# Wide high-part products in runs of eight, and activation slots 32 bytes longer, in a split-fp32 decoder trunk

## The chip, the cores and the metric

The kernel runs on one core of a Trainium2 chip. The metric is the time of one execution on the device in microseconds, as the median of several runs. The kernel before the change was run three times: 1990.41, 1990.26 and 1989.77 us, median 1990.26.

## What is computed

One recurrent layer (RG-LRU) and one sliding-window attention layer with sinks, each followed by a SwiGLU feed-forward block, over a residual stream of 256 tokens by 2048 features in float32. Nearly all the arithmetic is in matrix products of the activations (256 tokens) with weights:

```
h = rms_norm(x, g1);  y, xb = split(h @ lru_w_in)           # 2048 x 4096
xb = conv4(xb);  r, i = sigmoid(blockdiag(xb))               # 8 blocks of 256 x 256, twice
x = x + (lru_scan(r, i, xb) * gelu(y)) @ lru_w_out           # 2048 x 2048
x = x + (silu(gate) * up) @ ffn_w_out                        # 2048 x 11264, 5632 x 2048
k, v = split(rms_norm(x) @ w_kv)                             # 2048 x 512
x = x + attention(rms_norm(x) @ w_q, k, v, sinks) @ w_o      # 2048 x 2048, twice
x = x + (silu(gate) * up) @ ffn_w_out                        # second feed-forward block
```

## The kernel before, in words

**Layout.** Activations are kept transposed: features on the 128 partitions, the 256 tokens along the free axis, so a feature tile is 128 x 256. Weights are the stationary operand, 128 x 128 at a time, and activations stream past them as the moving operand.

**Split products.** To come near float32 with the one-pass type float32r, every operand is split in a high part, rounded to float32r, and a low part, the rest. A product is then three: weight high by activation high, weight high by activation low, weight low by activation high. A split activation lies in a *slot* of 512 columns: the high part in columns 0 to 255, the low part in 256 to 511. There are 58 slots, allocated one after the other in the same pool (`slot`, L138), and handed out and taken back in a queue. Other 256-wide temporaries use slots too.

**Jobs.** Weights come in blocks of 128 x 1024 float32 (512 KB): two feature tiles (k = 0, 1) by four output tiles (f = 0 to 3). One block is one job. `stream` (L271) walks the list of all jobs: it loads a block four jobs ahead on SyncE's queue into one of four `raw` buffers (L241), splits it three jobs ahead into `hi` on ScalarE (L259) and `lo` on VectorE (L260), again with four buffers each, and issues the job's products on TensorE. 688 of the jobs are jobs of `group` (L340); 8 are gate jobs with their own loop (L641) and 8 are K/V jobs (L832 to L843).

**Products of a job.** `group` makes a list of (k, f, part), and `products` (L289) issues it at L323, or at L321 where the product is to be held behind other matmuls. Parts are named in `PARTS` (L287):

```
PARTS = {"h": (1, 0, 2 * T), "a": (1, 0, T), "b": (1, T, 2 * T), "l": (0, 0, T)}
```

Part a is weight high by the slot's high half and b by its low half, both 256 wide and summed into the same 256 columns of a PSUM bank. Part h is both at once, 512 wide: it needs the whole bank, the two halves of which are added when the bank is evicted. Part l is weight low by the high half. So a job has 24 narrow products, or 16 if all a and b are taken as h. A bank that takes an h part is called *two* here. In each group two of the four banks are two (three in the query projection, `wide=3`; none where `sync` is empty or the group is *paired*, which is so for 16 jobs of the attention's output projection, where two output tiles share a bank).

**Order.** In before, most products are a, b and l. `products` takes three h parts in a row at certain jobs of a group (`SYNC`, L63), at its start, and after matmuls of other kinds (`pe_other`, L327, which norms, scores and transposes go through; `RUNS`, `since` and `due`, L301 to L314). The last job of a group goes output tile by output tile, so that banks finish one after the other. In the middle of a job, and at its end, `half_tick` and `run_bg` issue steps of the background work (evictions' further steps, norms, gates, softmax), as far as a running estimate of the time of VectorE and ScalarE allows.

**Evictions.** `pull` (L387) and `residual` (L469) take a bank. If it is two, ScalarE copies the second half to a temporary (L113, `t<-b`) and VectorE adds it to the first (L122); otherwise one operation of VectorE or ScalarE does. At the end of the kernel the residual tiles are stored as they are finished (L481).

Of the kernel before, what the change touches and what calls it, by code (L numbers as in the profile page):

```python
# [17 lines left out]
P = 128  # L18
D = 2048
T = 256  # L20
# [20 lines left out]
class Val:  # L41


    def __init__(self, ap=None):
        self.ap = ap
        self.ready = False


class Trunk:
# [11 lines left out]
    DEBT = 2500.0  # L61
    WARM = 15
    SYNC = (0, 2, 5)  # L63
    RUNS = 3
    DVE_TICK = 640.0
    ACT_TICK = 800.0

    def __init__(self, ctx, tc, dram):
        self.tc, self.nc, self.d = tc, tc.nc, dram
        nc = self.nc  # L70
        const = ctx.enter_context(tc.tile_pool(name="const", bufs=1))
        psum = ctx.enter_context(tc.tile_pool(name="psum", bufs=1, space=bass.MemoryType.PSUM))
        tmp = ctx.enter_context(tc.tile_pool(name="tmp", bufs=1))
        self.tmp = tmp
        self.par = const.tile([P, NPAR], F32, name="par")
        self.con = const.tile([P, NCON], F32, name="con")
        self.cc = const.tile([P, 32], F32, name="cc")
        self.x = [const.tile([P, 4, T], F32, name=f"x{i}") for i in range(4)]
        self.slots = deque(range(58))
        self.spool = const  # L80
        self.held = {}
        self.raw = [const.tile([P, 1024], F32, name=f"raw{i}") for i in range(4)]
        self.hi = [const.tile([P, 1024], F32R, name=f"hi{i}") for i in range(4)]
        self.lo = [const.tile([P, 1024], F32R, name=f"lo{i}") for i in range(4)]
        self.banks = deque(psum.tile([P, 512], F32, name=f"b{i}") for i in range(8))
        self.misc = 0
        self.started = False
        self.xin = 0
        self.other = None
        self.runs = 0  # L90
        self.since = 0
        self.hold = False
        self.tmps = deque(const.tile([P, T], F32, name=f"t{i}") for i in range(4))
        self.halves = deque(const.tile([P, T], F32, name=f"h{i}") for i in range(8))
        self.rstd = [const.tile([P, T + 2], F32, name=f"rstd{i}") for i in range(2)]
        self.acc = const.tile([P, T], F32, name="acc")
        self.sq = deque(const.tile([P, T], F32, name=f"sq{i}") for i in range(2))
        self.jobs = []
        self.bg = deque()
        self.tick = -2 * self.LD  # L100
        self.dve = 0.0
        self.act = 0.0
# [36 lines left out]

    def slot(self, dt=F32R):  # L140
        i = self.slots.popleft()
        s = self.spool.tile([P, 2 * T], dt, tag=f"s{i}", name=f"s{i}")
        self.held[id(s)] = (i, s)
        return s

# [143 lines left out]
    def products(self, todo, st, hi, lo, x2, last, keep=False, paired=False):  # L289

        ps, begun = st["ps"], st["begun"]
        rest, half, n = list(todo), len(todo) // 2, 0
        ticked = False
        while rest:
            if not ticked and n >= half and not (self.since == 0 and rest[0][2] == "h"):
                self.half_tick()
                ticked = True  # L300
            if self.other is not None:  # L301
                self.runs = self.RUNS
            if not keep and self.runs and rest[0][2] != "h":
                left = set(rest)
                run = [(k, f) for k in range(2) for f in range(4) if ps[f][1] and (k, f, "a") in left
                       and (k, f, "b") in left][:3]
                new = ps[rest[0][1]][1] and ps[rest[0][1]][2] not in begun
                due = self.other is not None or self.since % 3 == 1 and self.since > 3
                if len(run) == 3 and (new or due and ps[run[0][1]][2] in begun):
                    self.runs -= 1  # L310
                    rest = [(k, f, "h") for k, f in run] + [q for q in rest if q[:2] not in run or q[2] == "l"]
            k, f, p = rest.pop(0)
            n += 1 + (p == "h")
            self.since = 0 if p == "h" else self.since + 1  # L314
            high, c0, c1 = self.PARTS[p]
            w = (hi if high else lo)[:, k * 512 + f * P:k * 512 + f * P + P]
            args = (ps[f][0][:, 0:c1 - c0], w, x2[k][:, c0:c1])
            kw = dict(start=ps[f][2] not in begun, stop=last and all(q[1] != f for q in rest), skip_group_check=paired)
            if self.other is not None and p == "h":
                with self.tc.issue_after(self.other):  # L320
                    self.nc.tensor.matmul(*args, **kw)  # L321
            else:
                self.nc.tensor.matmul(*args, **kw)  # L323
            self.other = None
            begun.add(ps[f][2])
# [14 lines left out]
    def group(self, src, nk, xs, done, last=False, sync=(), paired=False, jobs=None, wide=2):  # L340

        st = {}
        jobs = self.jobs if jobs is None else jobs
        both = [(k, f) for k in range(2) for f in range(4)]
        for c in range(nk // 2):
            def mm(hi, lo, c=c):
                if c == 0:
                    if paired:  # L350
                        ps = [self.bank() for _ in range(2)]
                        st["ps"] = [(ps[f // 2][:, f % 2 * T:f % 2 * T + T], False, f // 2, f % 2) for f in range(4)]
                        st["bank"] = ps
                    else:
                        ps = [self.bank() for _ in range(4)]
                        st["ps"] = [(p, bool(sync) and f < wide, f, 1) for f, p in enumerate(ps)]
                        st["bank"] = ps
                    st["begun"] = set()
                    self.hold = False
                elif c >= nk // 2 - 2:  # L360
                    self.hold = True
                x2 = [self.need(xs[2 * c + kt]) for kt in range(2)]
                keep = not self.started
                if keep:
                    self.started = True
                    todo = [(k, f, p) for k in range(2) for q in ("ab", "l") for f in range(4)
                            for p in ("h" if q == "ab" and k == 0 and f < 2 else q)]
                elif c == nk // 2 - 1:

                    todo = [(k, f, p) for f in range(4) for k in range(2) for p in "abl"]  # L370
                else:
                    if c in sync:
                        self.runs = max(self.runs, 1)

                    two = [f for f in range(4) if st["ps"][f][1]]
                    one = [f for f in range(4) if f not in two]
                    order = [(one, "ab"), (one, "l")] + [(two, q) for q in (("ab", "l") if c == 0 else ("l", "ab"))]
                    todo = [(k, f, p) for g, q in order for k in range(2) for f in g for p in q]
                self.products(todo, st, hi, lo, x2, c == nk // 2 - 1, keep, paired)
                if last:  # L380
                    for q in x2:
                        self.free(q)
                if c == nk // 2 - 1:
                    done([(p, two, st["bank"][b] if last_of else None) for p, two, b, last_of in st["ps"]])
            jobs.append((src(c), mm))

    def pull(self, bank, o=None, r=None):  # L387
# [743 lines left out]
```

## Time and profile before

| | |
|---|---|
| median of the three runs | 1990.26 us |
| span of the profiled execution, first to last instruction | 1988.6 us |
| TensorE busy | 1982.0 us, 16684 matmuls |
| VectorE busy | 1271.2 us |
| ScalarE busy | 1067.9 us |
| weights and inputs read | 371.88 MB, 188 GB/s over the span |

The profile is of one execution. PE stands for TensorE's matmuls, PEld for its weight loads, DVE for VectorE, ACT for ScalarE and SP for SyncE; L323 is line 323 of the kernel. A row of a group names line, engine and operation, the output and inputs by the program's names (numbers left out), the shape and the count; behind the bar stand its busy time in us, the mean ns of one, and the idle time of the engine just before. In a row of a stretch (two times from the span's start, with a colon) stand its length, then for each engine the busy time and the number of instructions, and the granted clock (1.00 is full). In a row of the timeline stand the start in us, the time from the first start to the last end, and the count of like instructions in a row. Matmuls are pipelined: the duration of one is its latency, and the next starts long before it ends.

### The profile page before, as it was taken

To read this page: it belongs to the slowest core of one execution; us is meant where nothing else is said; L and a number is where in the kernel's file an instruction comes from. 1 tells how busy PE (TensorE), PEld (TensorE's weight loads), DVE (VectorE), ACT (ScalarE), POOL (GpSimd) and SP (SyncE) were. 2 spreads that over 40 slices of the span, in tenths; PEclk is the share of its full clock that TensorE was granted. 3 is DMA by queue.
4 is the path that set the end of the run, shared out by engine and by line. 5 is a ranking of instruction groups with operands and counts; after the bars stand their busy time and mean duration, and the time that the engine had idled before them with its cause. 6 is when DMAs were issued, how large, how long until landed. Compare 5 with 4: busy or idle time off the path is not lost.

```text
span 1988.6 us, 40066 instructions
## 1 busy us (share of the span) xinstructions
PE 1982.0 (100%) x16684; PEld 1935.5 (97%) x16684; DVE 1271.2 (64%) x2049; ACT 1067.9 (54%) x1624; POOL 0.2 (0%) x4
## 2 busy tenths in 40 slices
PE   9999999999999999999999999999999999999999
PEld 9999999999999999999999889999999999999999
DVE  8988876556556655545668786755565565554453
ACT  7798655444444444444556775544454454444442
POOL 0000000000000000000000000000000000000000
PEclk9999999999999999999999999999999999999999
DMA  8555655565556555556555435565566656656663
GB/s 279 185 187 182 211 191 192 196 196 191 192 195 196 191 192 196 195 191 194 197 186 167 134 101 163 188 197 195 191 193 196 195 191 194 197 193 203 204 208 128
DMA packets 105302, 376.58 MB, mean 189 GB/s; under 512 B 11808, under 2 KB 14240, under 8 KB 105120
## 3 DMA queue, kind: packets, MB, share of 16 engines
q1 hardware_dynamic: 104832, 373.88, 57.8%
q8 instruction: 130, 2.13, 0.4%
q14 instruction: 52, 0.43, 0.1%
q10 hardware_dynamic: 288, 0.14, 0.0%
HBM read 371.88 MB, written 2.10 MB: 188 GB/s over the span
## 4 chain that ended last, share of the span: by engine, by line
PE 99%; ACT 0%; DVE 0%; DMA 0%; issue 0%; ACTq 0%
PE b L323 94%; PE b L334 2%; PE b L641 1%; PE b L331 1%; PE b L832 1%; ACT s L113 0%; PE b L321 0%; PE b L841 0%; PE b L842 0%; PE b L843 0%; DMA x<-in_x 0%; DVE s L131 0%; DVE lo L260 0%; ACT L113 0%; DVE s L122 0%
## 5 line engine op out<-in xcount | busy, mean ns | idle before, releaser
L323 PE MATMUL b<-s,hi 128*128 128x256 f32 (+1 forms) x10276 | 1431.9, 285 | 0.4 <-ACT s L113 0.4
L323 PEld LDWEIGHTS b<-s,hi 128*128 128x128 f32 x10276 | 1313.4, 188 | 30.4 <-ACT s L113 0.7
L260 DVE TENSOR_TENSOR lo<-raw,hi 128x1024 fp32r<-128x1024 f32 (+1 forms) x705 | 861.4, 1223 | 651.2 <-ACT hi L259 648.1
L259 ACT ACTIVATE hi<-raw 128x1024 fp32r<-128x1024 f32 (+1 forms) x705 | 745.7, 1059 | 817.7 <-PE b L323 756.7
L323 PE MATMUL b<-s,lo 128*128 128x256 f32 x5504 | 831.8, 277 | 0.0
L323 PEld LDWEIGHTS b<-s,lo 128*128 128x128 f32 x5504 | 720.4, 188 | 2.4 <-issue 0.8
L113 ACT ACTIVATE s<-h 128x256 fp32r<-128x256 f32 (+1 forms) x106 | 40.8, 411 | 23.8 <-DVE h L122 23.8
L113 ACT ACTIVATE t<-b 128x256 f32<-128x256 f32 x136 | 49.8, 374 | 2.5 <-PE b L323 0.3
L113 ACT ACTIVATE s<-x,par 128x256 fp32r<-128x256 f32 x80 | 38.6, 499 | 19.3 <-DVE x L122 13.6
L113 ACT ACTIVATE s<-s 128x256 f32<-128x256 f32 (+1 forms) x112 | 39.6, 409 | 5.7 <-DVE s L126 5.5
L113 ACT ACTIVATE h<-h 128x256 f32<-128x256 f32 (+1 forms) x104 | 38.8, 375 | 2.1
L113 ACT ACT_TABLE_LOAD x30 | 38.5, 1283 | 0.5
L126 DVE SCALAR_TENSOR_TENSOR s<-x,par,s 128x256 fp32r<-128x256 f32 x80 | 37.5, 482 | 1.4 <-ACT s L113 0.8
L122 DVE TENSOR_TENSOR h<-b,rstd 128x256 f32<-128x256 f32 x100 | 37.6, 417 | 0.0
L122 DVE TENSOR_TENSOR x<-x,b 128x256 f32<-128x256 f32 x64 | 24.1, 418 | 21.0 <-PE b L323 21.0
L113 ACT ACTIVATE s<-s,h 128x128 f32<-128x128 f32 x64 | 28.3, 443 | 13.3 <-DVE h L131 13.2
L122 DVE TENSOR_TENSOR h<-h,rstd 128x256 f32<-128x256 f32 x94 | 35.4, 419 | 0.0
L122 DVE TENSOR_TENSOR h<-h,h 128x256 f32<-128x256 f32 x88 | 35.0, 420 | 0.4 <-ACT h L113 0.4
L122 DVE TENSOR_TENSOR s<-h,s 128x256 fp32r<-128x256 f32 x88 | 35.2, 420 | 0.1
L122 DVE TENSOR_TENSOR h<-b,t 128x256 f32<-128x256 f32 x92 | 34.6, 417 | 0.0
L122 DVE TENSOR_TENSOR s<-s,s 128x256 fp32r<-128x256 f32 (+1 forms) x80 | 30.9, 422 | 3.5 <-ACT s L113 3.5
L334 PE MATMUL b<-s,s 64*128 64x256 f32 (+3 forms) x292 | 29.0, 302 | 0.1
(99 smaller groups left out, 566.4 us busy)
## 6 DMA issues: line engine op xcount, KB each, us to landing
raw<-in_ffn_in SPq DMA_DIRECT2D x352, 512.0 KB, 3.5
raw<-in_ffn_out SPq DMA_DIRECT2D x176, 512.0 KB, 4.3
raw<-in_lru_in SPq DMA_DIRECT2D x63, 512.0 KB, 3.6
raw<-in_lru_out SPq DMA_DIRECT2D x32, 512.0 KB, 3.7
raw<-in_w_q SPq DMA_DIRECT2D x32, 512.0 KB, 3.3
raw<-in_w_o SPq DMA_DIRECT2D x32, 512.0 KB, 3.3
raw<-in_gate SPq DMA_DIRECT2D x8, 512.0 KB, 3.9
raw<-in_kv SPq DMA_DIRECT2D x8, 512.0 KB, 4.3
```

The lines of the kernel that those rows point to most:

```text
L113: self.nc.scalar.activation(out, in_, func, **kw)
L122: self.nc.vector.tensor_tensor(out, a, b, op)
L126: self.nc.vector.scalar_tensor_tensor(out, a, s, b, op0, op1)
L259: self.nc.scalar.activation(hi[:, q], raw[:, q], AF.Copy)
L260: self.nc.vector.tensor_tensor(lo[:, q], raw[:, q], hi[:, q].bitcast(F32), ALU.subtract)
L323: self.nc.tensor.matmul(*args, **kw)
L331: self.other = self.ins(f(*args, **kw))
L334: self.other = self.ins(f(*args, **kw))
L641: nc.tensor.matmul(out[j], (hi if high else lo)[:, c:c + P], x2[kt][:, q:q + T], start=kt == 0 and high > q, stop=kt == 1 and not high)
L832: nc.tensor.matmul(ps[f][:, 0:T], w0, x2[kt][:, q:q + T], start=k0 + kt == 0 and high > q, stop=k0 + kt == ND - 1 and not high)
```

## The change

All banks of groups that aren't paired become two, all their a and b parts become h parts, and a job issues its eight h parts first (k = 0 for the four output tiles, then k = 1) and then its eight l parts in the same order. The last job of a group goes output tile by output tile, two h and two l each. The runs of three and what decided on them are gone. A slot is allocated 520 columns long, of which 512 are used, so that slots lie 2080 bytes apart instead of 2048. The half-tick comes after half of the list, now eight h parts.

```diff
@@ class Trunk
-    RUNS = 3
+    STEP = 8
@@ slot
-        s = self.spool.tile([P, 2 * T], dt, tag=f"s{i}", name=f"s{i}")
+        w = self.spool.tile([P, 2 * T + self.STEP], dt, tag=f"s{i}", name=f"s{i}")
+        s = w[:, 0:2 * T]
@@ products
-            if not ticked and n >= half and not (self.since == 0 and rest[0][2] == "h"):
+            if not ticked and n >= half:
                 self.half_tick()
                 ticked = True
-            if self.other is not None:
-                self.runs = self.RUNS
-            if not keep and self.runs and rest[0][2] != "h":
-                left = set(rest)
-                run = [(k, f) for k in range(2) for f in range(4) if ps[f][1] and (k, f, "a") in left
-                       and (k, f, "b") in left][:3]
-                new = ps[rest[0][1]][1] and ps[rest[0][1]][2] not in begun
-                due = self.other is not None or self.since % 3 == 1 and self.since > 3
-                if len(run) == 3 and (new or due and ps[run[0][1]][2] in begun):
-                    self.runs -= 1
-                    rest = [(k, f, "h") for k, f in run] + [q for q in rest if q[:2] not in run or q[2] == "l"]
             k, f, p = rest.pop(0)
-            n += 1 + (p == "h")
-            self.since = 0 if p == "h" else self.since + 1
+            n += 1
@@ group
-                        st["ps"] = [(p, bool(sync) and f < wide, f, 1) for f, p in enumerate(ps)]
+                        st["ps"] = [(p, True, f, 1) for f, p in enumerate(ps)]
...
-                    todo = [(k, f, p) for k in range(2) for q in ("ab", "l") for f in range(4)
-                            for p in ("h" if q == "ab" and k == 0 and f < 2 else q)]
+                    todo = [(k, f, p) for k in range(2) for p in "hl" for f in range(4)]
+                elif paired:
+                    todo = [(k, f, p) for q in ("ab", "l") for k in range(2) for f in range(4) for p in q]
                 elif c == nk // 2 - 1:
-                    todo = [(k, f, p) for f in range(4) for k in range(2) for p in "abl"]
+                    todo = [(k, f, p) for f in range(4) for p in "hl" for k in range(2)]
                 else:
-                    if c in sync:
-                        self.runs = max(self.runs, 1)
-                    two = [f for f in range(4) if st["ps"][f][1]]
-                    one = [f for f in range(4) if f not in two]
-                    order = [(one, "ab"), (one, "l")] + [(two, q) for q in (("ab", "l") if c == 0 else ("l", "ab"))]
-                    todo = [(k, f, p) for g, q in order for k in range(2) for f in g for p in q]
+                    todo = [(k, f, p) for p in "hl" for k in range(2) for f in range(4)]
```

More of the change, by code (lines that the diff above doesn't have):

```diff
@@ L89, in __init__ @@
         self.other = None
-        self.runs = 0
-        self.since = 0
         self.hold = False
```

## The prediction

> **What bounds the kernel now.** I read the page first (busy shares, granted clock, chain), then TensorE's waits, then the matmul groups with their shapes kept apart, and then single stretches. The forecast hangs on the pitch, the time from one product's start to the next, and no group states it.
>
> ```profile
> span 1988.6 us, 40066 instructions
> PE 1982.0 (100%) x16684; PEld 1935.5 (97%) x16684; DVE 1271.2 (64%) x2049; ACT 1067.9 (54%) x1624; POOL 0.2 (0%) x4
> PEclk9999999999999999999999999999999999999999
> PE 99%; ACT 0%; DVE 0%; DMA 0%; issue 0%; ACTq 0%
> ```
>
> TensorE is busy for the whole span at full clock, and 99% of the chain that ended last is TensorE. This is what it waited for, in total:
>
> ```profile
> PE b L334 <- DVE s L131: 1.7, 3, 1.0
> PE b L268 <- DVE lo L265: 1.2, 1, 1.2
> PE b L323 <- ACT s L113: 0.4, 1, 0.4
> ```
>
> It waited 3.3 us in 1988.6, so no wait is there to be removed: the time can change only if the matmuls take more or less time, or if the change makes new waits. The matmuls by shape:
>
> ```profile
> L323 PE MATMUL b<-s,hi 128*128 128x256 f32 x9570 | 1291.3, 277 | 0.4 <-ACT s L113 0.4
> L323 PE MATMUL b<-s,lo 128*128 128x256 f32 x5504 | 831.8, 277 | 0.0
> L323 PE MATMUL b<-s,hi 128*128 128x512 f32 x706 | 201.6, 393 | 0.0
> ```
>
> The 277 ns of a narrow product is its latency, not its pitch: they overlap. For the pitch I take stretches that hold nothing but narrow products:
>
> ```profile
> 157.00:183.00 26.00, 26.00 (x223) 26.00 (x222) 22.49 (x43) 24.13 (x48) 0.00 (x0) 1.00 0.57 185
> 1890.00:1980.00 90.00, 90.00 (x797) 90.00 (x796) 41.29 (x38) 34.63 (x34) 0.00 (x0) 1.00 0.55 177
> ```
>
> A product is counted if any of its 277 ns falls into the stretch, which is 277/113, some 2.4 products too many. So 90.00/794.6 = 113.3 ns, and 26.00/220.6 = 117.9 ns. Clock and shape are the same in both: there is a **short rhythm** of 113.3 and a **long rhythm** of 117.9, 4.6 ns apart, and each holds for many products in a row. Which one holds can be seen to depend on where the operands start. In the shared K/V projection, L832 streams an activation slot past weights 12 times, and then L841 to L843 stream weights past an activation slot 12 times:
>
> ```profile
> 1013.80 0.39 PE L832 MATMUL b<-s,hi 128*128 128x256 f32 x2
> ...
> 1015.16 0.28 PE L841 MATMUL b<-hi,s 128*128 128x256 f32 x1
> ...
> 1016.58 0.40 PE L832 MATMUL b<-s,hi 128*128 128x256 f32 x2
> ...
> 1018.00 0.28 PE L841 MATMUL b<-hi,s 128*128 128x256 f32 x1
> ...
> 1019.37 0.39 PE L832 MATMUL b<-s,hi 128*128 128x256 f32 x2
> ...
> 1020.73 0.28 PE L841 MATMUL b<-hi,s 128*128 128x256 f32 x1
> ...
> 1022.14 0.40 PE L832 MATMUL b<-s,hi 128*128 128x256 f32 x2
> ```
>
> The first column is the start in us. Twelve products take 1.36, 1.42, 1.42, 1.37, 1.36, 1.41 us, that is 113, 118, 118, 114, 113, 118 ns each. Each time the moving operand goes from slot to weight tile the rhythm flips, and going back it stays: half of this stretch is in the long rhythm. As allocated, every slot starts 32 bytes past a multiple of 512 and every weight tile 480 past one. In the L323 products all moving operands lie at one offset, and there the rhythm holds.
>
> **The change part by part.** *Wide instead of two narrow.* Of the 688 jobs of L323, the 672 that aren't paired now issue 8 wide and 8 narrow low products: 5376 wide ones in place of 10752 narrow or fewer (719 are wide already: 706 above and, by the built program, 13 at L321). A pair costs 2 x 113.3 = 226.6. The latency of a wide product is 393 - 277 = 116 ns more than that of a narrow one; if the added columns cost as much in the pitch, a wide one takes 113.3 + 116 = 229.3 ns. Two places check this, three wide and two narrow products up to the start of the next piece, in the short and in the long rhythm:
>
> ```profile
> 361.90 1.07 PE L323 MATMUL b<-s,hi 128*128 128x512 f32 x5
> 362.81 0.39 PE L323 MATMUL b<-s,lo 128*128 128x256 f32 x2
> ...
> 185.76 1.10 PE L323 MATMUL b<-s,hi 128*128 128x512 f32 x5
> 186.69 0.52 PE L323 MATMUL b<-s,lo 128*128 128x256 f32 x3
> ```
>
> (0.91 - 2 x 0.1133)/3 = 228 ns, and (0.93 - 2 x 0.1179)/3 = 231 ns. I take 229.3, which lies between: +2.7 each, 5376 x 2.7 = 14.5 us, less 719 x 2.7 = 1.9 paid already: **+12.6 us**. The bounds: above, a wide product as slow as two in the long rhythm, 235.8; below, no row shows columns streamed faster than in the short rhythm, so I mirror the one difference that the trace shows and let a wide product save 4.6 on its pair, 222.0, or, further out, 4.6 on each of its halves, 217.4.
>
> Runs of three is all that the trace has. What the fourth to eighth do, it doesn't show; the bounds hold that too.
>
> *Slots 2080 bytes apart instead of 2048.* The moving operand's offset now takes 16 values in 512 bytes, and it changes four times in a job, between the two feature tiles of the high and of the low products and to the next job. No row shows an offset of 32 bytes to another slot; the nearest are the K/V rows, where a change of offset left half the products in the long rhythm. I take that half for all narrow products that remain with a slot as an operand: 5504 low ones, 256 of the paired jobs, 192 at L641, 192 of K/V, together 6144. 6144 x 0.5 x 4.6 = **+14.1 us**; ends: none in the long rhythm (0) and all (28.3). What is in it now has to come off. Most of it lies early:
>
> ```profile
> 20.00:320.00 300.00, 300.00 (x2519) 295.20 (x2518) 257.96 (x471) 223.17 (x377) 0.00 (x0) 1.00 0.61 197
> L323 PE MATMUL b<-s,hi 128*128 128x512 f32 x101 | 28.7, 392 | 0.0
> ```
>
> (The second row is of the same stretch.) 300.00 - 2519 x 0.1133 - 101 x 0.116 = 2.9 us: **-3 us**.
>
> *Evictions.* All four banks of a group now carry two halves, where it was two or three of four: about 137 more copies on ScalarE and as many adds on VectorE.
>
> ```profile
> L113 ACT ACTIVATE t<-b 128x256 f32<-128x256 f32 x136 | 49.8, 374 | 2.5 <-PE b L323 0.3
> L122 DVE TENSOR_TENSOR x<-x,b 128x256 f32<-128x256 f32 x64 | 24.1, 418 | 21.0 <-PE b L323 21.0
> ```
>
> That is 137 x 0.374 = 51 us on ScalarE (54% busy) and 137 x 0.42 = 58 us on VectorE (64%), spread over the span beside matmuls. The tightest place is the stretch 20 to 320 above: VectorE is busy 258 of 300 us, and eight groups with two more adds each bring 16 x 0.42 = 6.7 us against 42 us of idle time. I cost it at nothing; with that cover gone it would be those 7 us. Only the end has nothing beside it. The last group had single halves, and its last product was followed by one add:
>
> ```profile
> 1985.18 0.28 PE L323 MATMUL b<-s,lo 128*128 128x256 f32 x1
> 1985.49 0.42 DVE L122 TENSOR_TENSOR x<-x,b 128x256 f32<-128x256 f32 x1 [0.26 <-PE b L323]
> ```
>
> Now ScalarE copies the second half during that add (374 under 418 ns), and a second add follows: **+0.4 us** before the last store. Removed runs of three, the later half-tick (after 8 of 16 products, two thirds of a job) and the dropped order after other matmuls move background work by less than a job; weights, loads and queues stay as they are, and nothing waits for them now: 0.
>
> *Sum:* 12.6 + 14.1 - 3 + 0.4 = +24.1. The span was 1988.6, and the median of the runs, 1990.26, lies 1.7 above it: 1988.6 + 24.1 + 1.7 = **2014 us**. Own range: 228 and none in the long rhythm give 5376 x 1.4 - 1.9 - 3 + 0.4 = +3, 1993; 235.8 and all in it give 5376 x 9.2 - 1.9 + 28.3 - 3 + 0.4 = +73, 2063. Since neither end goes with the other term's middle, I cut it to 2003 to 2042.
>
> **The rivals.** *A: a toll per product, which the padding and the width take away.* If the 113.3 holds a fixed cost for each start, a wide product pays it once; and if the equal offsets are what keeps narrow products at 113.3 or 117.9, spreading them may help. With a toll of 4.6, wide 222.0, narrow all at 113.3: -5376 x 4.6 = -24.7, -1.9 (the 719 of now), -3, +0.4 = -29, **1961 us**; with the toll gone from narrow ones too it is lower, by up to 28 us. With the other terms as forecast (14.1 - 1.9 - 3 + 0.4 = 9.6 us) it decides once a wide product comes below 226.6 - 1.8 = 224.8 ns. For it speaks that offsets matter at all; against it 393 - 277 = 116, more than a narrow pitch, and the rows of three wide ones. The Trainium skill, TensorE: Matmul & The Clock Gate, section Back-to-back issue gap, speaks for it: an isolated warm product takes its columns at 2.4 GHz and 2.5 ns on top, so 215.8 ns wide and 109.2 narrow. By the difference alone, 2.5 ns a pair, the estimate would be -13.4 us, 1977; this trace's narrow pitch of 113.3 doesn't agree with that page's figure.
>
> *B: the padding does nothing.* Wide at 229.3, narrow all at 113.3: 12.6 - 3 + 0.4 = +10, **2000 us**. Against it, the K/V rows; for it, that a step of 32 bytes isn't the step seen there. The Trainium skill, SBUF — State Buffer, section Who interferes with whom, says that TensorE never waits for anyone there, by which offsets would be free: B again, and the K/V rows disagree with it.
>
> *C: a long rhythm throughout.* Every change of offset breaks the short rhythm and eight narrow products are too few to find it: wide 235.8, narrow 117.9, **2063 us**. For it: the long rhythm held for 220 products once it was there.
>
> That the edit doesn't do what it says can be left out: the built program has the 5376 wide products and the 2080-byte step.
>
> **How the numbers follow.** Forecast 0.38, A 0.33, B 0.17, C 0.06, and 0.06 that the terms cancel, within 0.2% (about what a measurement of this kernel can tell from no change, here 4 us). So slower 0.38 + 0.17 + 0.06 = 0.61, same 0.06, faster 0.33. The range leaves out most of C and the deeper part of A, where narrow products gain too, some 0.06 and 0.13: 1948 to 2042.
>
> **What would show it.** In the profile after, TensorE stays at 100% with waits of a few us. The wide group has about 5367 rows at L310 and some at L308. A stretch inside an FFN gives the job's pitch: now 24 x 113.3 = 2.72 us; by the forecast 8 x 229.3 + 8 x 115.6 = 2.76; by A 2.68; by B 2.74; by C 2.83. The low products of one job alone tell the rhythm: 0.91 us for eight at the short pitch, 0.94 at the long one. ScalarE's t<-b group grows from 136 to about 270. The forecast is wrong if the job is below 2.72, or if the added time lies in TensorE's waits instead of its pitch.

## The result and the profile after

The changed kernel takes 2042.64 us (median of 4 runs, 2042.49 to 2042.81) against 1990.3 us before: 1.0262 times the time, 95% interval 1.0248 to 1.0277. The forecast was 2014 us in a range of 1948 to 2042, so the sign was right and the added time, 52 us instead of 24, twice what was forecast and just outside the range. The page of the changed kernel, answering to the first lines of before:

```profile
span 2041.0 us, 31024 instructions
PE 2032.5 (100%) x12027; PEld 1776.5 (87%) x12027; DVE 1324.0 (65%) x2193; ACT 1104.7 (54%) x1761; POOL 0.2 (0%) x4
PEclk9999999999999999999999999999999999999999
```

TensorE is busy throughout at full clock as before. Its waits, in total:

```profile
PE b L321 <- DVE s L129: 1.7, 3, 1.0
PE b L267 <- DVE lo L264: 1.2, 1, 1.2
PE b L310 <- DVE s L124: 1.1, 1, 1.1
PE b L318 <- ACT h L111: 0.3, 1, 0.3
PE b L318 <- DVE s L120: 0.2, 1, 0.2
```

That is 4.5 us where it was 3.3: no engine became a new bound, and the time went into the products themselves. The groups by shape (L310 is now the products' line) show the 5367 wide and 5504 narrow low products, each some ns longer than in before (395 and 281 ns, where it was 393 and 277):

```profile
L310 PE MATMUL b<-s,hi 128*128 128x512 f32 x5367 | 1392.0, 395 | 1.1 <-DVE s L124 1.1
L310 PE MATMUL b<-s,lo 128*128 128x256 f32 x5504 | 796.4, 281 | 0.0
```

As before, the pitch says more than the duration. In the timeline of TensorE inside a feed-forward block each job is two pieces:

```profile
601.84 2.02 PE L310 MATMUL b<-s,hi 128*128 128x512 f32 x8
603.70 1.13 PE L310 MATMUL b<-s,lo 128*128 128x256 f32 x8
604.66 2.03 PE L310 MATMUL b<-s,hi 128*128 128x512 f32 x8
606.53 1.10 PE L310 MATMUL b<-s,lo 128*128 128x256 f32 x8
607.47 2.03 PE L310 MATMUL b<-s,hi 128*128 128x512 f32 x8
```

From start to start: 1.86 and 1.87 us for eight wide products, 233 ns each, and 0.96 and 0.94 us for eight narrow ones, 119 ns each. A job is 2.81 us, where 24 products of 113.3 took 2.72.

Taken from start to start over the whole trace, without the steps that hold a wait or a matmul of another kind, the mean pitch is:

| | narrow, ns | wide, ns | above 113.3 and 226.7, us in all |
|---|---|---|---|
| before | 113.7 | 229.5 | 5.0 + 2.0 = 7.0 |
| after | 117.9 | 232.4 | 27.6 + 30.5 = 58.1 |

The last column is what all products together take beyond the short rhythm, narrow ones first. It grew by 51.1 us, 22.6 on the narrow and 28.5 on the wide products. With 0.9 us at the end (below) that is 52.0 of the 52.4 us between the two spans, 1988.6 and 2041.0. So nearly the whole loss is pitch.

### The profile page after: what moved, and what is told of

Its sections match the earlier page's. It is cut to its first block, busy times and chain, and to the rows that moved or that the text cites. A ratio compares the mean times of both kernels' runs of the same rounds, so it can differ in the third digit from the quotient of the medians.

```text
span 2041.0 us, 31024 instructions
## 1 busy us (share of the span) xinstructions
PE 2032.5 (100%) x12027; PEld 1776.5 (87%) x12027; DVE 1324.0 (65%) x2193; ACT 1104.7 (54%) x1761; POOL 0.2 (0%) x4
## 5 line engine op out<-in xcount | busy, mean ns | idle before, releaser
L310 PE MATMUL b<-s,hi 128*128 128x512 f32 (+1 forms) x5623 | 1426.7, 390 | 1.1 <-DVE s L124 1.1
L310 PEld LDWEIGHTS b<-s,hi 128*128 128x128 f32 x5623 | 979.6, 188 | 163.2 <-DVE s L124 1.4
L310 PEld LDWEIGHTS b<-s,lo 128*128 128x128 f32 x5504 | 774.4, 188 | 79.6 <-issue 0.8
L310 PE MATMUL b<-s,lo 128*128 128x256 f32 x5504 | 796.4, 281 | 0.0
L111 ACT ACTIVATE t<-b 128x256 f32<-128x256 f32 x280 | 103.4, 380 | 89.4 <-PE b L310 57.9
L120 DVE TENSOR_TENSOR h<-b,t 128x256 f32<-128x256 f32 x192 | 80.1, 419 | 0.9 <-ACT t L111 0.3
L120 DVE TENSOR_TENSOR h<-h,rstd 128x256 f32<-128x256 f32 x194 | 77.0, 420 | 1.5
L881 DVE CUSTOM_DVE_ANT_0 s<-b,con,par 128x128 f32<-128x128 f32 x64 | 27.1, 473 | 0.0
```

The lines of the kernel that those rows point to most:

```text
L111: self.nc.scalar.activation(out, in_, func, **kw)
L120: self.nc.vector.tensor_tensor(out, a, b, op)
L881: nc.vector.tensor_tensor_reduce(sc[hh][:, c0:c1], ps[hh][:, c0:c1], con[:, K_MASK + c0:K_MASK + c1], rr[:, b * 8 + f * 2 + hh:b * 8 + f * ...
```

## The experiments

Four theories were tested. Runs are called by the first part of their label, e1 to e16. **P**: changes of the operand's offset between products, which the padding brings, throw the products out of the short rhythm. **W**: a run of eight wide products costs by itself. **D**, formed after the first runs: the pitch hangs on the distance between the start of the moving operand and that of the weights, modulo 256 bytes. **M**, at first and then as M2: wide products go round a cycle of three pitches, and what rhythm follows depends on the count modulo three. Each run stands beside runs of the kernel before on the same chip.

**Width alone.**

```diff
-    STEP = 8          # of the changed kernel
+    STEP = 0
```

> The change without its padding: slots 2048 bytes apart again, all high-part products wide, eight and eight. Theory P (the offsets that vary from slot to slot throw the products out of the short rhythm): narrow pitch back to 113.3 ns, wide near 229, time about 2000 us. Theory W (a run of eight wide products costs by itself and leaves the narrow ones behind it in the long rhythm, whatever the offsets): wide 231 to 233 ns, narrow 117 to 118, time 2030 to 2045 us.

Measured: 2012.8 us, 1.0113 (1.0098 to 1.0128). The two theories each missed: the time lies between them. Its timeline shows why:

```profile
605.02 2.00 PE L310 MATMUL b<-s,hi 128*128 128x512 f32 x8
606.86 1.07 PE L310 MATMUL b<-s,lo 128*128 128x256 f32 x8
607.76 1.99 PE L310 MATMUL b<-s,hi 128*128 128x512 f32 x8
609.59 1.11 PE L310 MATMUL b<-s,lo 128*128 128x256 f32 x8
610.53 1.31 PE L310 MATMUL b<-s,hi 128*128 128x512 f32 x5
```

Eight narrow products take 0.90 us in one job (113 ns) and 0.94 in the next (118 ns), by turns. Of some 580 whole jobs half have a narrow mean of 113 to 114 ns and half one of 117 to 119, and the wide ones go 226, 229, 232 ns, over and over, 229.0 in the mean. Products beyond the short rhythm: 27.7 us, so +20.7 against before; the spans differ by 2010.6 - 1988.6 = 22.0.

**Padding alone.**

```diff
-        s = self.spool.tile([P, 2 * T], dt, tag=f"s{i}", name=f"s{i}")
+        w = self.spool.tile([P, 2 * T + 8], dt, tag=f"s{i}", name=f"s{i}")
+        s = w[:, 0:2 * T]
```

> The kernel before with nothing but the padding: slots 2080 bytes apart, products in the old order. P: narrow pitch about 118 ns in all L323 products, 15,000 x 4.6 ns = 69 us more, about 2055 us. W: the old time within 5 us, 1990 us.

Measured: 2060.43 us, 1.0353 (1.0337 to 1.0368): P's number, and W as the only cause is out. Narrow products have 118.1 ns in the mean. In the order of before, the padding costs 70 us.

**One common offset, another one.**

```diff
+        self.gap = const.tile([P, 8], F32, name="gap")   # 32 bytes ahead of the slots
```

> The kernel before with 32 unused bytes ahead of the slots: all slots still 2048 bytes apart and at one common offset, but 64 instead of 32 bytes past a multiple of 512, while the weight tiles stay at 480. If only a change of offset between products costs (P in its plain form): short rhythm as before, 113.3 ns, 1990 us. If the common offset itself sets the pitch: the narrow pitch moves as a whole, to anything between 108 and 118 ns, 1910 to 2055 us.

Measured: 2088.91 us, 1.0495 (1.048 to 1.0511). All slots still lie at one common offset here, and it is the slowest run of all, so P in its plain form falls: the offset itself matters. A stretch of 55 us near the end that holds only narrow products, in before and in this run:

```profile
1925.00:1980.00 55.00, 55.00 (x488) 55.00 (x487) 25.20 (x25) 20.44 (x20) 0.00 (x0) 1.00 0.51 166
```

```profile
2025.00:2080.00 55.00, 55.00 (x461) 55.00 (x460) 20.83 (x17) 18.05 (x17) 0.00 (x0) 1.00 0.44 144
```

These are 488 products against 461; less the 2.4 that reach in from before, 113.3 and 119.9 ns.

Traffic of the other engines isn't the reason. In the whole trace of this run a narrow product takes 119.8 ns in the mean where neither VectorE nor ScalarE runs beside it (2340 of them) and 120.0 where both do (3551); it takes 119.9 where no DMA packet is under way (3044) and 119.9 where more than twelve are (7232).

**Steps of 64 bytes.** `STEP = 16` in the changed kernel, with one temporary less of two kinds to make room.

> The change with slots 2112 bytes apart, a step of 64 bytes instead of 32 (one temporary fewer of two kinds to make room). P with any change of offset harmful: as the changed kernel, 2035 to 2050 us. P with only odd multiples of 32 bytes harmful: narrow near 113.3, wide near 229, about 2000 us. W: 2030 to 2045 us.

Measured: 2039.24 us, 1.0246 (1.0229 to 1.0263), as with 32 bytes. Odd multiples of 32 bytes aren't what is wrong.

**Weights and slots moved together**, the 32 bytes of e3 ahead of both (before `raw` in the list of tiles):

> The kernel before with 32 unused bytes ahead of weights and slots alike: slots 64 and weight tiles 0 past a multiple of 512, so that their distance stays what it was. If the distance between the moving operand's offset and the weights' sets the pitch: 113.3 ns and 1990 us as before. If the slots' own offset does (64 past, as in the run before in which they alone were moved and the narrow pitch was 120.4 ns): 120 ns and 2085 to 2090 us.

Measured: 1990.49 us, 1.0001 (0.999 to 1.0011). Moved by the same 32 bytes together with the weights, the slots cost nothing: the absolute offset doesn't matter, the distance between the two operands does. **Other distances**, the gap of e3 with other lengths:

> The kernel before with all slots moved by 256 bytes, to 288 past a multiple of 512; weights at 480. In the run with nothing but the padding, the products with a slot at 288 were the shortest (116.6 ns mean, 113 at the shortest quarter). If the pattern repeats every 256 bytes and only changes between products kept them from the short rhythm: 113.3 ns, 1990 us. If the distance to the weights matters in the whole 512 bytes: another pitch, 116 to 121 ns, 2030 to 2090 us.

> The kernel before with all slots moved by 448 bytes, to 480 past a multiple of 512, the same offset as the weights. By the runs so far no theory names a number; if every distance but the old one costs, 117 to 121 ns and 2040 to 2090 us. A pitch under 113 ns would show that the old distance is not the best one and give a version that beats both.

> The kernel before with all slots moved by 128 bytes: 160 past a multiple of 512, weights at 480, so 192 bytes behind the weights' offset modulo 256 where it was 64. So far a distance of 64 gave 113.3 ns, 0 gave 119.9 and 96 gave 120.4. Theory D (the pitch hangs on this distance modulo 256): any one pitch for the whole run; in the shared K/V projection, where the operands change roles and the distance is 192 too, both 113 and 118 ns were seen, so 113.3 and 1990 us is the likeliest, 118 and 2060 us the other end.

> The kernel before with all slots moved by 64 bytes, distance 128 modulo 256. Distances of 0, 96 and 192 gave 119.9, 120.4 and 117.8 ns, 64 gave 113.3. Theory D says one pitch for the run without naming it; 117 to 121 ns, 2050 to 2090 us, if 64 is the only good distance. If the padding's 70 us are the mean over the eight distances, the eight base runs must average near 2060 us; a mean well below it would leave a price for the changes themselves.

> The kernel before with all slots moved by 96 bytes, distance 160 modulo 256. As in the run with distance 128: 117 to 121 ns, 2050 to 2090 us, if 64 is the only good distance; below 113 ns if there is a better one.

> The kernel before with all slots moved by 160 bytes, distance 224 modulo 256. As in the run with distance 128: 117 to 121 ns, 2050 to 2090 us, if 64 is the only good distance; below 113 ns if there is a better one.

> The kernel before with all slots moved by 224 bytes, distance 32 modulo 256. As in the run with distance 128: 117 to 121 ns, 2050 to 2090 us, if 64 is the only good distance; below 113 ns if there is a better one.

In before, slots start at 32 and weights at 480 past a multiple of 512, a distance of 64 modulo 256. With the mean pitch of a stretch of 55 us of narrow products near the end, counted as above:

| distance mod 256, bytes | run | median, us | pitch, ns |
|---|---|---|---|
| 0 | e7 | 2087.25 | 119.9 |
| 32 | e16 | 2045.22 | 116.6 |
| 64 | before, e5, e6 | 1990.3 to 1990.5 | 113.3 |
| 96 | e3 | 2088.91 | 119.9 |
| 128 | e13 | 2070.49 | 118.6 |
| 160 | e14 | 2051.59 | 117.4 |
| 192 | e9 | 2054.09 | 117.9 |
| 224 | e15 | 2064.78 | 118.4 |

Two of the expectations are missed: for a distance of 192 the likeliest was said to be 1990 us, and e16 lies below its 2050. The pitch is a mean: at 64 every step of the stretch takes 112 to 114 ns, at 96 they vary from 116 to 125.

The row of e6, 256 bytes on, is that of before again, and that of e16 is the nearest of the others:

```profile
1925.00:1980.00 55.00, 55.00 (x488) 55.00 (x487) 25.27 (x25) 20.44 (x20) 0.00 (x0) 1.00 0.54 166
```

```profile
1980.00:2035.00 55.00, 55.00 (x474) 55.00 (x473) 23.18 (x20) 19.11 (x18) 0.00 (x0) 1.00 0.49 161
```

D holds: moved by 256 bytes, 0.9999 (0.9989 to 1.001); moved by anything else that was tried, 1.0275 or more. Of the eight distances that the padding's steps of 32 bytes produce, the kernel before sits on the only one at 113.3. None lies below it, so no layout among these gives a version that beats before. The mean of the eight medians (with 1990.3 for 64) is 2056.6 us; padding alone measured 2060.4. So the sum agrees with the mean of the distances to about 4 us. Product by product it doesn't: where the trace of e2 is matched with the addresses of the built program, narrow products at 64 take 117.0 ns, not 113.3, and those at 0 take 118.6, not 119.9. In a mix, the products at the good distance lose it, and others gain.

**Changes between distances.** One slot in eight longer by 256 or by 128 bytes, in the kernel before:

```diff
-        s = self.spool.tile([P, 2 * T], dt, tag=f"s{i}", name=f"s{i}")
+        w = self.spool.tile([P, 2 * T + 64 * (i % 8 == 3)], dt, tag=f"s{i}", name=f"s{i}")   # or 32 *
+        s = w[:, 0:2 * T]
```

> The kernel before with one slot in eight 256 bytes longer, so that slots lie at 32 or at 288 bytes past a multiple of 512 and products change between the two. Theory D: nothing changes modulo 256, 113.3 ns and 1990 us. Theory P (every change of offset from one product to the next throws them out of the short rhythm): 116 to 118 ns, 2030 to 2060 us.

> The kernel before with one slot in eight 128 bytes longer: slots at 32, 160, 288 and 416, distances of 64 and 192 modulo 256. If each of the two distances by itself holds 113.3 ns (see the run with all slots moved by 128), then D says 1990 us, and anything above it is the price of a change between two good distances: with P 2030 to 2060 us.

Measured: 1990.01 us, 1.0 (0.9989 to 1.001), and 2042.27, 1.0262 (1.0241 to 1.0282). Changes by 256 bytes cost nothing, which P can't explain. The second run mixes distances of 64 and 192, which alone take 1990 and 2054; their mean is 2022 (2025.5 by the built program's share of each, as 55% of the narrow products lie at 192), and it takes 17 to 20 us more than that. Its products at a distance of 64 have 117.8 ns in the mean, and still 117.5 after thirty in a row at 64: after products at the wrong distance, those at the right one don't find the short rhythm again. Those at 192 take 116.3, less than the 117.7 of e9. So D as tested holds for one distance throughout; in a mix, a product's own distance doesn't tell its pitch, and a change between distances does cost where one of them is good, a remainder of P. The distance of 192 isn't good, and with that the condition under which the expectation named 1990 isn't met.

**How many wide products in a row.** Slots as in before, and six or five wide products at the head of a job; the rest of the high parts and a group's last job narrow:

```diff
-                    todo = [(k, f, p) for p in "hl" for k in range(2) for f in range(4)]
+                    todo = [(k, f, p) for q in ("ab", "l") for k in range(2) for f in range(4)
+                            for p in ("h" if q == "ab" and 4 * k + f < 6 else q)]   # or < 5
```

> The change without its padding, and six wide products at the head of a job instead of eight: the last two pairs are narrow, as are those of a group's last job. In the kernel before, runs of three wide products led back into the short rhythm; the run of eight without padding left 116.4 ns behind it. Theory M (a run whose length is a multiple of three ends where it began, in the short rhythm): narrow 113.3, wide 229, about 455 jobs or more x 6 x 2.3 = 6 to 9 us more than before, 1996 to 2000 us. Theory W (any long run leaves the long rhythm behind): narrow 116 to 118 ns, 2015 to 2035 us.

Measured: 2041.55 us, 1.0256 (1.0239 to 1.0274). M's time is missed, and W's upper end is passed too.

```profile
219.32 1.99 PE L310 MATMUL b<-s,hi 128*128 128x512 f32 x10
221.15 1.07 PE L310 MATMUL b<-s,lo 128*128 128x256 f32 x8
222.06 0.39 PE L310 MATMUL b<-s,hi 128*128 128x512 f32 x1
226.19 4.62 PE L310 MATMUL b<-s,hi 128*128 128x512 f32 x14 [3.74 <-DVE s L120]
230.64 1.10 PE L310 MATMUL b<-s,lo 128*128 128x256 f32 x8
...
601.38 2.02 PE L310 MATMUL b<-s,hi 128*128 128x512 f32 x10
603.24 1.10 PE L310 MATMUL b<-s,lo 128*128 128x256 f32 x8
604.18 2.02 PE L310 MATMUL b<-s,hi 128*128 128x512 f32 x10
606.04 1.10 PE L310 MATMUL b<-s,lo 128*128 128x256 f32 x8
606.98 2.02 PE L310 MATMUL b<-s,hi 128*128 128x512 f32 x10
```

(A piece of ten is six wide and four narrow products.) Up to 222 us M is right: all 50 whole jobs without a wait have narrow products at 113 ns, 0.91 us for eight, and wide ones at 226, 229, 232 ns. Then TensorE waits 3.7 us for VectorE in the middle of a run. After some products that take up to 428 ns each, at a granted clock of 0.57 from 226.2 to 229.5 us, comes the long rhythm, 0.94 us for eight low products, in all but four of the 458 whole jobs left. From start to start the wide ones then go 233, 236, 229, 231, 227, 229 ns in job after job. So runs of six keep the rhythm that they find, and M had looked only at a run that begins in the short one. That led to M2: in the long rhythm the narrow products advance the same cycle, so what counts is the number of both, and a job's six and twelve, both multiples of three, hand the next job the place that they were handed. M2 doesn't explain the 233 and 236 ns.

> The change without its padding and with five wide products at the head of a job, then three narrow pairs and eight low ones: 5 and 14. Theory M2 (wide products go round a cycle of three, narrow ones in the long rhythm too; a run adds its length modulo three): 5 and 14 leave 2 over three as 8 and 8 do, so jobs should alternate between narrow at 113.3 and at 118, mean 115.5, wide 229, time near that of the change without its padding, 2008 to 2018 us. Theory W (a long run of wide products leaves the long rhythm behind): narrow 117 to 118 in every job, 2035 to 2050 us, as with six.

Measured: 2016.79 us, 1.0133 (1.0116 to 1.015), with M2's alternation:

```profile
601.38 2.01 PE L310 MATMUL b<-s,hi 128*128 128x512 f32 x11
603.24 1.10 PE L310 MATMUL b<-s,lo 128*128 128x256 f32 x8
...
607.00 1.99 PE L310 MATMUL b<-s,hi 128*128 128x512 f32 x11
608.83 1.07 PE L310 MATMUL b<-s,lo 128*128 128x256 f32 x8
609.74 2.01 PE L310 MATMUL b<-s,hi 128*128 128x512 f32 x11
```

The eight low products of one job take 0.94 us, those of another 0.91; of some 510 whole jobs half are in the short rhythm and half in the long one. W, which put every job in the long rhythm at 2035 us or more, is missed. That the count goes by threes is a reading that fits eight and eight, five and fourteen, and six and twelve; no other counts were run.

## Why the prediction was wrong

**What bounds the kernel:** right. Nearly all of the added time is pitch, waits grew by a microsecond, and nothing else became a bound. Two terms of the sum failed, and both for what sets the rhythm.

**Wide products at 229.3 ns:** right for equal offsets (229.0 in the run with the width alone, so B's wide pitch held), wrong for the change. The step took its three rows from products at the one good distance and left them standing under the padding, whose price it put on narrow products alone. With the padding it is 232.4 ns. The term was forecast as +12.6 us and measured 30.5 - 2.0 = 28.5. That is the larger miss, 15.9 of the 28 us by which the forecast fell short.

**Half of the narrow products in the long rhythm, 14.1 us less the 3 of before:** the other step that failed, as the prediction put it, is "I take that half for all narrow products". The half came from the K/V rows, where the operands change roles. There the distance goes from 64 to -64, that is 192, so the rows show two fixed distances by turns, with both rhythms at each; they don't give odds for what the padding's eight distances do. Forecast were 11.1 us, measured 27.6 - 5.0 = 22.6, and two causes together make it: without any padding the runs of eight already put half of the jobs' narrow products into the long rhythm (115.9 ns mean, e1), and the padding's mix of distances takes the rest (117.9 ns; by the built program's addresses 116.9 for those at 64 and 116.7 to 118.7 for the others). The prediction had noted that the trace shows nothing of the fourth to eighth wide product and put no price on it beyond its bounds.

**A coincidence:** the width alone measures 2012.8 us with wide products at 229.0 and narrow ones at 115.9 ns, nearly the forecast's 2014, 229.3 and 115.6. But the forecast put the half in the long rhythm down to the padding, and that run has none.

**The sum split anew:** the width costs 2012.8 - 1990.1 = 22.7 us and the padding on top of it 2042.6 - 2012.8 = 29.8.

**Evictions:** they cost next to nothing in the middle, as forecast. The end was undersized:

```profile
2036.56 0.40 PE L310 MATMUL b<-s,lo 128*128 128x256 f32 x2
2036.64 0.42 DVE L120 TENSOR_TENSOR x<-x,t 128x256 f32<-128x256 f32 x1
2036.75 0.38 ACT L111 ACTIVATE t<-b 128x256 f32<-128x256 f32 x1 [0.32 <-DVE x L120]
2037.00 0.42 DVE L120 TENSOR_TENSOR x<-x,b 128x256 f32<-128x256 f32 x1
2037.34 0.96 DVE L120 TENSOR_TENSOR x<-x,t 128x256 f32<-128x256 f32 x2
2037.45 0.38 ACT L111 ACTIVATE t<-b 128x256 f32<-128x256 f32 x1 [0.32 <-DVE x L120]
```

The copy on ScalarE doesn't run beside the first add: it waits for VectorE's add each time (the releaser in brackets) and starts after that has ended. From the end of the last product to the end of the last add it is 2038.30 - 2036.96 = 1.34 us, where before it was 1985.91 - 1985.46 = 0.45: +0.9 instead of +0.4.

**The rivals.** A, the toll per product, is out: in no run do wide products have a mean below 229.0 ns, and neither the fewer products nor any layout tried was faster than before. The Trainium skill's 2.5 ns on top of an isolated product (TensorE: Matmul & The Clock Gate, Back-to-back issue gap) would have made a pair cost more than a wide product; here the wide one costs 2.3 ns more than a pair at 113.3, at the best distance. B, that the padding does nothing, is out by e2: it costs 70 us by itself. The Trainium skill's rule that TensorE never waits on anyone in SBUF (SBUF — State Buffer, Who interferes with whom) is about other engines, and e3's pitch agrees with it: it is 119.8 ns beside idle VectorE and ScalarE and 120.0 beside busy ones. But it doesn't follow that offsets are free, as the prediction read it: moving the slots by 32 bytes against the weights costs 99 us. C, the long rhythm throughout, came nearest, at 0.06, but as a mean: the narrow products have its 117.9, with steps from 112 to 128 ns where those of the long rhythm in before lie at 116 to 120, and the wide ones stayed below its 235.8.

## What to carry to other kernels

Where TensorE is the bound, read the pitch from start to start, stretch by stretch; durations hide it. Before padding or re-basing a tile that streams past weights, work out the distance between the two operands' start addresses and treat it as part of the design: here one distance in eight makes the kernel 2.7 to 5% faster than the others do. A rhythm that depends on what ran before can't be priced by its share of some stretch; find what switches it.

## What the runs showed of the hardware that wasn't expected

For one-pass float32r products of 128 x 128 weights with 256 columns, each with its own weights, each kept at one distance throughout, the mean pitch depends on the distance of the two operands' start addresses modulo 256 bytes: 113.3 ns at 64, 116.6 to 119.9 at the seven other multiples of 32. At a distance of 64 there is a second steady rhythm of 117.8 ns. It holds for 220 products in a row in before, and in e8 from a wait at 222 us on in all but four jobs. 512-column products run there in a cycle of 226, 229 and 232 ns (e1, e12, and e8 up to 222 us). Which rhythm follows a run of them depends on the counts: eight and eight, and five and fourteen, change between the two, six and twelve keep the one they find. Modulo three is a reading of these three counts. What in the chip makes the distance and the count matter stays open: the runs show the dependence, not its cause.
